# The weights' high and low tiles moved to sixteen places in a 256-byte line

## The chip, the cores and the metric

The kernel runs on one core of one Trainium2 chip. The metric is the device time of one execution in microseconds (us), lower is better. The profile is of one execution, taken by the hardware profiler; the times of the runs were taken without it.

## The reference

The program is a two-layer decoder over 256 tokens of width 2048, in float32: a Mamba-2 layer, a gated MLP with a short causal convolution, a shared key and value projection, an attention layer, and a second gated MLP. Nearly all of the arithmetic is products of the token matrix with weight matrices:

```python
zxbcdt = x @ w_in
...
u = causal_dwconv(x @ w_up, conv_w, conv_b)
gate, val = u[..., :D_FF], u[..., D_FF:]
return (jax.nn.silu(gate) * val) @ w_down
...
kv = h @ w_kv
...
q = (h @ w_q).reshape(Bsz, S, N_HEADS, HEAD_DIM).transpose(2, 0, 1, 3)
```

The inner widths are 10304 for `w_in`, 2 x 5632 for `w_up`, 4096 for `w_kv`, 2048 for the others.

## The kernel before

**High and low parts.** TensorE multiplies in its float32r form, which keeps fewer bits than float32. So every operand is held as two parts, the rounded value (high) and the rest (low), and a product is high x high + low x high + high x low. The activations stand in SBUF as `hT`, `yT`, `gT` or `aT`, 128 partitions with, for each block of 128 rows of the inner dimension, 256 high values (one for each token) and behind them 256 low ones.

**Steps.** The weights come in 880 pieces of 128 x 2 x 512 floats (512 KB, 4096 bytes in a partition), in the order in which they are used. One piece is one step. `load` (L171) issues its DMA into one of four `raw` buffers. `split` (L181) takes one buffer of tag `hi` and one of tag `lo` from the pool `wts`, which has four of each (L95, `LA + 1`), or, for a few steps, free space in `hT` (`spare`). Then ScalarE casts `raw` to the high part (L200) and VectorE subtracts it from `raw` for the low part (L201). `splits` (L204) keeps this up to three steps ahead of the step in work.

**Two kinds of matmul.** A chunk is a block of 512 output columns.

- In mode W, the weights are the stationary operand. `some` (L241) loads 128 x 128 of the high weights and streams high and low activations, 512 columns (L256), or loads 128 x 128 of the low weights and streams the high activations, 256 columns (L259). A piece gives eight of each line, and since every second step turns the order of the two parts round, 16 of one line follow each other; `paired` chunks put two pieces together, and there 32 do.
- In mode X, the activations are the stationary operand and the weights move, 512 columns at a time (256 in the last pieces of a matrix, where `half` is called with `piece`). `half` (L212) issues L222 with the high weights, L223 with the low weights, and L227 with the activations' low part and the high weights.
- One chunk, mode H, has the two parts of 64 columns side by side (`beside`, L262).

Each matmul comes with a weight load of its own: PEld in the profile is the load, PE the matmul.

**What sets the order.** The order of every engine's instructions is written out by hand (`tc.manual_schedule`, L99). The main loop (L1167) walks over the steps, and the dictionaries `pre`, `mid`, `post`, `inner` and `outer` hold the work to be issued around each step; `at(i, f)` puts `f` behind step `i`. Semaphores follow from the tiles that instructions share.

**Addresses.** A tile is a stretch of bytes that is the same in all partitions. The pool `base` lies first: `ident`, `mean`, `cols` (padded to a multiple of 64 floats, `LINE`), `hT`, then the small `mhalf` (8 bytes, for which 32 bytes are set aside), and behind it `tri` and the two buffers of `u`, among others. `wts` follows with four `raw`, four `hi` and four `lo` buffers of 4096 bytes each, then the four `t4k` buffers, then the pool of the stage (`mamba`, `ffn0`, `att`, `ffn1`). The large tiles are multiples of 256 bytes long, so `hT`, `raw`, `hi`, `lo`, `gT`, `yT`, `aT` and `kT` all begin at the same place in a line of 256 bytes, 128 bytes into it; `u` begins 32 bytes further. With the stage `mamba` open, 228,480 bytes of a partition are taken.

**The tile of squares.** In the Mamba stage, for each of eight groups, `x_turn` (L770) writes `xe` (L780), 2048 bytes, which the matmuls of `y_off` (L803) read. Later in the same group, `z_cut` (L829) writes `sq`, 2048 bytes as well, high part by ScalarE (L831) and low part by VectorE (L832), and the matmuls of `z_rms` (L838) read it. The step numbers from the group's start are 13 for `x_turn`, 18 for `y_off`, 22 for `z_cut`, 23 for `z_rms`; the next group starts 16 steps later.

Of the kernel before, what the change touches and what calls it, by code (L numbers as in the profile page):

```python
# [19 lines left out]
F32R = mybir.dt.float32r  # L20
# [4 lines left out]
P = 128  # L25
D = 2048
S = 256
# [12 lines left out]
NC = 512  # L40
# [19 lines left out]
def chunks():  # L60

    z, b, c, dt = 0, 2 * DI, 2 * DI + NG * DS, 2 * DI + 2 * NG * DS

    def some(mode, name, layer, c0, n, nk):
        return [(mode, name, layer, c0 + i * NC, nk, False) for i in range(n)]

    def ffn(layer):
        up = [some(m, "ffn_w_up", layer, c + j * NC, 1, KD)[0] for j in range(DFF // NC)
              for m, c in (("W" if j else "X", 0), ("W", DFF))]
        return up + some("X", "ffn_w_down", layer, 0, 4, KF)  # L70

    out = some("W", "mamba_w_in", 0, b, 2, KD)
    out[0] = out[0][:5] + (True,)
    out += some("H", "mamba_w_in", 0, dt, 1, KD) + some("W", "mamba_w_in", 0, c, 2, KD)
    for g in range(NG):
        out += some("W", "mamba_w_in", 0, DI + g * NC, 1, KD) + some("W", "mamba_w_in", 0, z + g * NC, 1, KD)
    out += some("X", "mamba_w_out", 0, 0, 4, DI // P) + ffn(0)
    out += some("X", "w_kv", None, D, 1, KD) + some("W", "w_kv", None, 0, 4, KD) + some("W", "attn_w_q", 0, 0, 4, KD)
    return out + some("X", "w_kv", None, D + NC, 3, KD) + some("X", "attn_w_o", 0, 0, 4, KD) + ffn(1)
# [12 lines left out]
def yoco_kernel(ctx: ExitStack, tc: tile.TileContext, x, lmg, lmb, lfg, lfb, x_t, columns, w, out):  # L92
    nc = tc.nc
    base = ctx.enter_context(tc.tile_pool(name="base", bufs=1))
    wts = ctx.enter_context(tc.tile_pool(name="wts", bufs=LA + 1))  # L95
# [30 lines left out]
    steps, plan = [], chunks()  # L126
# [44 lines left out]
    def load():  # L171
        i = pos["load"]
        if i >= n_steps:
            return
        pos["load"] += 1
        t = wts.tile([P, 2, NC], F32, tag="raw", name="raw", bufs=RAW)
        for e in (slice(0, 1), slice(1, 2)) if i == 0 else (slice(0, 2),):
            nc.sync.dma_start(t[:, e], w[i][:, e])
        raw_t[i] = t

    def split():  # L181
        i = pos["split"]
        pos["split"] += 1
        t = raw_t.pop(i)
        if i in spare:
            h, l = (bufs["h"][:, k:k + 2].rearrange("p k a t -> p k (a t)") for k in (spare[i], spare[i] + 2))
        else:
            h = wts.tile([P, 2, NC], F32R, tag="hi", name="hi")
            l = wts.tile([P, 2, NC], F32R, tag="lo", name="lo")
        hi_t[i], lo_t[i] = h, l  # L190
        if steps[i][0].mode == "H":
            for a, w in enumerate((h, l)):
                v = t[:, a].rearrange("p (k n) -> p k n", k=8)
                w = w.rearrange("p a (k e n) -> p (a k) e n", e=2, n=NC // 8)
                nc.scalar.copy(w[:, :, 0], v)
                nc.vector.tensor_sub(w[:, :, 1], v, w[:, :, 0].bitcast(F32))
            return load()
        for e in ((0,), (1,)) if i < 2 else ((0, 1),):
            sl = slice(e[0], e[-1] + 1)
            nc.scalar.copy(h[:, sl], t[:, sl])  # L200
            nc.vector.tensor_sub(l[:, sl], t[:, sl], h[:, sl].bitcast(F32))  # L201
        load()

    def splits(i, most=2):  # L204

        for _ in range(1 if steps[i][0] in calm else most):
            j = pos["split"]
            ahead = LA + 1 + sum(i <= k < j for k in spare)
            if j < min(i + ahead, n_steps) and (j in spare or sum(k not in spare for k in hi_t) < LA + 1):
                split()  # L210
# [151 lines left out]
    bufs = {"h": base.tile([P, KD, 2, S], F32R, name="hT")}  # L362
# [179 lines left out]
    def open_pool(name):  # L542
        g = tc.tile_pool(name=name, bufs=1)
        pool[name] = (g, g.__enter__())
        return pool[name][1]
# [26 lines left out]
    calm.append(chB[0])  # L572
    put_x(0)
    split()
    put_x(2)
    split()
    for p in range(2, 8):
        amid(p - 2, put_x, 2 * p)


    mp = open_pool("mamba")
# [123 lines left out]
    G = [dict() for _ in range(NG)]  # L705
# [121 lines left out]
        nc.vector.tensor_add(sz[:, 0], sz[:, 0], sz[:, 1])  # L827

    def z_cut(g):  # L829
        G[g]["sq"] = q = mp.tile([P, 2, S], F32R, tag="sq", name="sq", bufs=1)  # L830
        nc.scalar.copy(q[:, 0], G[g]["sz"][:, 0])  # L831
        nc.vector.tensor_sub(q[:, 1], G[g]["sz"][:, 0], q[:, 0].bitcast(F32))  # L832

# [40 lines left out]
    for g in range(NG):  # L874
# [22 lines left out]
        at(s0 + 20, z_square, g)  # L897
        at(s0 + 21, z_sum, g)
        at(s0 + 22, z_cut, g)
        at(s0 + 23, z_rms, g)  # L900
        at(s0 + 24, z_log, g)
# [217 lines left out]
    for h in range(HEADS):  # L1119
        i, j = divmod(h, 4)  # L1120
# [87 lines left out]
```

## Time and profile before

| | us |
|---|---|
| median of 2 runs | 2539.39 (2539.25 to 2539.53) |
| the profiled execution | 2539.57 |
| its span, first to last instruction | 2537.3 |
| TensorE (PE) busy | 2524.6 |
| weight loads (PEld) busy | 2197.0 |
| VectorE (DVE) busy | 1657.9 |
| ScalarE (ACT) busy | 1365.5 |

The rows that are quoted below come from the following views. The page's first part gives busy time, share of the span and count of each engine; its second part cuts the span in 40 slices of 63.4 us and gives the busy share in tenths. The chain of work that ended last is followed back from the last instruction, each step to what released it. A row of the groups by line reads: line, engine, operation, written tile, read tiles, partitions x elements, count, busy time in us, mean ns of one, then the engine's idle time before it with what ended it. A row of the order of time reads: start in us, time in us from the first start to the last end of so many (x32) merged instructions, engine, line, operation. A matmul's own time overlaps the next one's, so the distance of starts is what counts. A row of one tile's instructions gives duration in ns as min/median/max, then the first and the last start in us. A row of a stretch gives its length, then for PE, PEld, DVE, ACT and POOL the busy us and the count, the granted TensorE clock, the DMA share and GB/s.

### The profile page before, as it was taken

How to read it: one execution, taken by the hardware profiler on the slowest of the kernel's cores; microseconds unless marked ns; L12 is line 12 of the kernel's file. 1: busy time of each engine (PE TensorE's matmuls, PEld its weight loads, DVE VectorE, ACT ScalarE, POOL GpSimd, SP SyncE). 2: the span in 40 equal slices, each digit the busy share in tenths (PEclk: the TensorE clock that was granted, in tenths of full speed). 3: DMA queues.
4: the chain of work that ended last, by engine and by line, in shares of the span. 5: the costliest groups of instructions: out<-in, count | busy, mean ns of one | idle time of the engine just before them, and what ended most of it. 6: DMA issues, size and time to landing. Idle time of an engine off the chain costs nothing.

```text
span 2537.3 us, 36085 instructions
## 1 busy us (share of the span) xinstructions
PE 2524.6 (100%) x13983; PEld 2197.0 (87%) x13983; DVE 1657.9 (65%) x2140; ACT 1365.5 (54%) x1790; POOL 76.6 (3%) x96
## 2 busy tenths in 40 slices
PE   9999999999999999999999999999999999999998
PEld 8888888888888888888888888888888888888887
DVE  7778778755666766666445646645767676765545
ACT  6677787643465555554334445543555555554333
POOL 0000000000200000000000200000200000000001
PEclk9999999999999999999999999999999999999999
DMA  7666665666665555556676655456655555566664
GB/s 253 202 194 199 205 194 186 196 208 223 213 202 189 190 188 189 191 183 200 204 235 203 209 194 168 159 180 227 221 187 193 191 187 190 183 199 200 199 227 163
DMA packets 141739, 502.59 MB, mean 198 GB/s; under 512 B 15856, under 2 KB 16368, under 8 KB 141568
## 3 DMA queue, kind: packets, MB, share of 16 engines
q1 hardware_dynamic: 136448, 482.92, 58.2%
q0 software_dynamic: 4832, 16.85, 2.1%
q8 instruction: 109, 1.79, 0.3%
q14 instruction: 62, 0.51, 0.1%
q10 hardware_dynamic: 288, 0.52, 0.1%
HBM read 491.77 MB, written 8.45 MB: 197 GB/s over the span
## 4 chain that ended last, share of the span: by engine, by line
PE 99%; DMA 0%; DVE 0%; SPq 0%; issue 0%; ACT 0%
PE acc L256 40%; PE acc L259 21%; PE acc L222 11%; PE acc L223 11%; PE acc L227 11%; PE acc L794 1%; PE tp L396 0%; PE tp L227 0%; PE tp L223 0%; PE tp L222 0%; DMA raw<-in_w 0%; PE tp L803 0%; PE acc L777 0%; PE tp L1073 0%; PE tp L1107 0%; PE tp L1099 0%
## 5 line engine op out<-in xcount | busy, mean ns | idle before, releaser
L201 DVE TENSOR_TENSOR lo<-raw,hi 128x1024 fp32r<-128x1024 f32 (+1 forms) x869 | 1059.9, 1225 | 749.6 <-ACT hi L200 616.6
L200 ACT CAST hi<-raw 128x1024 fp32r<-128x1024 f32 (+1 forms) x869 | 908.6, 1048 | 857.8 <-PE acc L227 371.9
L256 PE MATMUL acc<-hT,hi 128*128 128x512 f32 x4480 | 1059.4, 391 | 1.1 <-ACT hi L200 1.1
L256 PEld LDWEIGHTS acc<-hT,hi 128*128 128x128 f32 x4480 | 828.4, 188 | 166.0 <-ACT hi L200 2.0
L259 PEld LDWEIGHTS acc<-hT,lo 128*128 128x128 f32 x4480 | 562.8, 191 | 15.8 <-issue 1.2
L259 PE MATMUL acc<-hT,lo 128*128 128x256 f32 x4480 | 570.6, 283 | 0.0
L223 PE MATMUL acc<-lo,gT 128*128 128x512 f32 (+1 forms) x678 | 254.5, 378 | 0.0
L222 PE MATMUL acc<-hi,gT 128*128 128x512 f32 (+1 forms) x678 | 254.1, 377 | 0.0
L227 PE MATMUL acc<-hi,gT 128*128 128x512 f32 (+1 forms) x678 | 200.7, 377 | 0.0
L222 PEld LDWEIGHTS acc<-hi,gT 128*128 128x128 f32 x678 | 127.6, 188 | 23.2
L223 PEld LDWEIGHTS acc<-lo,gT 128*128 128x128 f32 x678 | 127.6, 188 | 23.1
L227 PEld LDWEIGHTS acc<-hi,gT 128*128 128x128 f32 x678 | 124.8, 188 | 23.8
L223 PE MATMUL acc<-lo,yT 128*128 128x512 f32 (+1 forms) x270 | 98.6, 369 | 0.0
L222 PE MATMUL acc<-hi,yT 128*128 128x512 f32 (+1 forms) x270 | 98.5, 369 | 0.0
L222 PE MATMUL acc<-hi,hT 128*128 128x512 f32 x192 | 78.8, 410 | 0.0
L227 PE MATMUL acc<-hi,yT 128*128 128x512 f32 (+1 forms) x270 | 77.7, 369 | 0.0
L223 PE MATMUL acc<-lo,hT 128*128 128x512 f32 x192 | 75.4, 393 | 0.0
L599 DVE TENSOR_TENSOR u<-u,acc 128x512 f32<-128x512 f32 x108 | 73.4, 681 | 2.3 <-ACT u L598 1.4
L626 DVE SCALAR_TENSOR_TENSOR g<-u,cols,g 128x254 f32<-128x254 f32 (+1 forms) x176 | 73.3, 478 | 0.7 <-ACT g L621 0.7
L626 DVE SCALAR_TENSOR_TENSOR v<-u,cols,v 128x254 f32<-128x254 f32 (+1 forms) x176 | 73.0, 477 | 0.0
L1023 ACT CAST gT<-v 128x512 fp32r<-128x512 f32 x44 | 27.3, 621 | 84.5 <-DVE v L1022 84.5
L458 POOL TENSOR_TENSOR rs<-rs,mhalf 128x1 f32<-128x1 f32 x8 | 7.5, 932 | 2002.2 <-DVE nb L459 2002.2
(223 smaller groups left out, 1911.3 us busy)
## 6 DMA issues: line engine op xcount, KB each, us to landing
raw<-in_w SPq DMA_DIRECT2D x880, 512.0 KB, 3.6
mA<-acum_d POOLq DMA_DIRECT2D x16, 512.0 KB, 6.4
hres<-r POOLq DMA_DIRECT2D x12, 512.0 KB, 6.7
r<-hres SPq DMA_DIRECT2D x12, 512.0 KB, 4.9
eA<-acum_d POOLq DMA_DIRECT2D x16, 128.0 KB, 7.5
r<-in_x SPq DMA_DIRECT2D x4, 512.0 KB, 5.1
gb<-in_ln_mix_g SPq DMA_DIRECT2D x8, 256.0 KB, 4.8
gb<-in_ln_mix_b SPq DMA_DIRECT2D x8, 256.0 KB, 5.0
```

The source lines that it names most:

```text
L200: nc.scalar.copy(h[:, sl], t[:, sl])
L201: nc.vector.tensor_sub(l[:, sl], t[:, sl], h[:, sl].bitcast(F32))
L222: nc.tensor.matmul(a, th, h[:, kk, sl], start=k == 0, stop=False)
L223: nc.tensor.matmul(a, th, l[:, kk, sl], start=False, stop=False)
L227: nc.tensor.matmul(a, ch.x.lo(k)[:, ts], h[:, kk, sl], start=False, stop=k == ch.nk - 1)
L256: nc.tensor.matmul(banks[j], w[:, kk, js], ch.x.both(k), start=begins, stop=ends, skip_group_check=True)
L259: nc.tensor.matmul(banks[j][:, :S], w[:, kk, js], ch.x.hi(k), start=begins, stop=ends, skip_group_check=True)
L458: nc.gpsimd.tensor_tensor(self.rs[:, h, :], self.rs[:, h, :], mhalf[:, 0, :], op=OP.pow)
L599: nc.vector.tensor_add(dst, dst, p[:, :, :S])
L626: nc.vector.scalar_tensor_tensor(d, u[:, i % 2, :S - k], c1(self.at_w, w[n - 1 - k] + self.ia + i), d, op0=OP.mult, op1=OP.add)
L794: nc.tensor.matmul(ps[64 * q:64 * q + 64, c, j * P:(j + 1) * P], G[g]["xdt"][:, c, h * 64:(h + 1) * 64], G[g]["A", c][:, h, :], start=True ...
L1023: nc.scalar.copy(h, v[:, sl])
```

## The change

Every `hi` and `lo` buffer becomes 2 x 512 + 32 floats long, 4224 bytes in place of 4096. The tile that is used in it begins `at` floats in, where `at` is 0, 4, 8 ... 28 and goes on by 4 floats (16 bytes) every second step. Since 4224 is 16 lines of 256 bytes and a half, neighbouring buffers are also half a line apart, so that with both, sixteen steps in a row stand at sixteen places of a line, all of them multiples of 16 bytes. The high and the low part of a step are at the same place. The chunk of mode H uses `at` 0, and the steps in `spare` are not touched. Then `sq` no longer has a buffer of its own and takes the tag of `xe`, whose single buffer the two now share; this gives back 2048 bytes in a partition, where the eight longer buffers take 1024. All tiles behind `wts` lie 1024 bytes further, at the same place in a line as before. The order of the instructions on every engine and the semaphores that they wait for are the same in both kernels.

```diff
@@ -185,8 +185,10 @@
         if i in spare:
             h, l = (bufs["h"][:, k:k + 2].rearrange("p k a t -> p k (a t)") for k in (spare[i], spare[i] + 2))
         else:
-            h = wts.tile([P, 2, NC], F32R, tag="hi", name="hi")
-            l = wts.tile([P, 2, NC], F32R, tag="lo", name="lo")
+
+            at = 4 * (i // 2 % 8) if steps[i][0].mode != "H" else 0
+            h, l = (wts.tile([P, 2 * NC + 32], F32R, tag=n, name=n)[:, at:at + 2 * NC].rearrange("p (a n) -> p a n", a=2)
+                    for n in ("hi", "lo"))
         hi_t[i], lo_t[i] = h, l
         if steps[i][0].mode == "H":
             for a, w in enumerate((h, l)):
@@ -827,7 +829,7 @@
         nc.vector.tensor_add(sz[:, 0], sz[:, 0], sz[:, 1])
 
     def z_cut(g):
-        G[g]["sq"] = q = mp.tile([P, 2, S], F32R, tag="sq", name="sq", bufs=1)
+        G[g]["sq"] = q = mp.tile([P, 2, S], F32R, tag="xe", name="sq", bufs=1)
         nc.scalar.copy(q[:, 0], G[g]["sz"][:, 0])
         nc.vector.tensor_sub(q[:, 1], G[g]["sz"][:, 0], q[:, 0].bitcast(F32))
```

## The prediction

> **What bounds the kernel now.** I read the page's busy shares first, then the chain of work that ended last, then the order of time on TensorE in one stretch of each of the two kinds of matmul.
>
> ```profile
> PE 2524.6 (100%) x13983; PEld 2197.0 (87%) x13983; DVE 1657.9 (65%) x2140; ACT 1365.5 (54%) x1790; POOL 76.6 (3%) x96
> ...
> DVE  7778778755666766666445646645767676765545
> ...
> PEclk9999999999999999999999999999999999999999
> ...
> PE 99%; DMA 0%; DVE 0%; SPq 0%; issue 0%; ACT 0%
> PE acc L256 40%; PE acc L259 21%; PE acc L222 11%; PE acc L223 11%; PE acc L227 11%; PE acc L794 1%; PE tp L396 0%; PE tp L227 0%; PE tp L223 0%; PE tp L222 0%; DMA raw<-in_w 0%; PE tp L803 0%; PE acc L777 0%; PE tp L1073 0%; PE tp L1107 0%; PE tp L1099 0%
> ```
>
> The reader is to see that 99% of the chain is TensorE, that its clock is granted in full, and that five lines hold 94%: L256 and L259, where the weights are the stationary operand, and L222, L223 and L227, where they are the moving one. A busy TensorE need not be at its peak, so the next question is what sets the distance from one matmul to the next. First a stretch of the first kind, then one of the second:
>
> ```profile
> 2000.48 4.00 PE L259 MATMUL acc<-hT,lo 128*128 128x256 f32 x32
> 2004.31 7.44 PE L256 MATMUL acc<-hT,hi 128*128 128x512 f32 x32
> 2011.59 4.00 PE L259 MATMUL acc<-hT,lo 128*128 128x256 f32 x32
> 2015.42 0.86 PE L256 MATMUL acc<-hT,hi 128*128 128x512 f32 x3
> ```
>
> ```profile
> 1206.36 0.61 PE L227 MATMUL acc<-hi,gT 128*128 128x512 f32 x2
> ...
> 1207.72 0.39 PE L227 MATMUL acc<-hi,gT 128*128 128x512 f32 x1
> ```
>
> 32 low-part matmuls of 256 columns take 2004.31 - 2000.48 = 3.83 us, 119.7 ns each, and again 3.83 us from 2011.59. Of the second kind, six of 512 columns take 1207.72 - 1206.36 = 1.36 us, 226.7 ns each. So 256 more columns cost 107.0 ns, 0.418 ns a column, and what is left over is 119.7 - 107.0 = **12.7 ns for each matmul, whatever its width**. The high-part run of 32 takes 2011.59 - 2004.31 = 7.28 us, 227.5 ns each, nearly the same. The four buffers of the weights take turns through these runs, so nothing above the place in a line shows in the distance.
>
> **What the change does, part by part.** Order, waits, sizes, shapes and DMAs of every instruction stay as they were; only addresses move. Each high and low tile becomes 1056 floats long, 4224 bytes = 16 lines of 256 + 128 bytes, so neighbouring buffers stand half a line apart, and the data begins another 16 x (step // 2 mod 8) bytes in. That gives sixteen places, all multiples of 16 bytes, where before all tiles began at one. These groups count what is touched:
>
> ```profile
> L201 DVE TENSOR_TENSOR lo<-raw,hi 128x1024 fp32r<-128x1024 f32 (+1 forms) x869 | 1059.9, 1225 | 749.6 <-ACT hi L200 616.6
> L200 ACT CAST hi<-raw 128x1024 fp32r<-128x1024 f32 (+1 forms) x869 | 908.6, 1048 | 857.8 <-PE acc L227 371.9
> L256 PEld LDWEIGHTS acc<-hT,hi 128*128 128x128 f32 x4480 | 828.4, 188 | 166.0 <-ACT hi L200 2.0
> L259 PEld LDWEIGHTS acc<-hT,lo 128*128 128x128 f32 x4480 | 562.8, 191 | 15.8 <-issue 1.2
> L222 PE MATMUL acc<-hi,gT 128*128 128x512 f32 (+1 forms) x678 | 254.1, 377 | 0.0
> L222 PE MATMUL acc<-hi,yT 128*128 128x512 f32 (+1 forms) x270 | 98.5, 369 | 0.0
> L222 PE MATMUL acc<-hi,hT 128*128 128x512 f32 x192 | 78.8, 410 | 0.0
> L222 PE MATMUL acc<-hi,aT 128*128 128x512 f32 (+1 forms) x126 | 46.9, 376 | 0.0
> L222 PE MATMUL tp<-hi,gT 128*128 128x256 f32 x72 | 18.7, 282 | 0.0
> ```
>
> *Weight loads of L256 and L259*: 2 x 4480 = 8960 reads of 512 bytes. *Moving reads of L222, L223 and L227*: 678 + 270 + 192 + 126 + 72 = 1338 on each line, 4014 reads of 1 or 2 KB. Together 12,974 of the 13,983 matmuls read something moved. No row of before has a TensorE read at another place, so the cost has to be bounded. Below nothing: a gain can at most take the 12.7 ns that isn't columns. Above: a read that begins inside some unit of the memory touches one unit more. Places are multiples of 16 bytes, so a unit of 16 costs nothing, and with a unit of 64 bytes, 12 of 16 places pay. For a moving read that is 16 columns, 16 x 0.418 = 6.7 ns. For a weight load it is one unit in eight of a stream that repeats every 119.7 ns, at most 15.0 ns, and only where the load has no slack: a load begins with each matmul, and in L256's runs it has 227.5 - 119.7 = 107.8 ns to spare, so only L259's 4480 can show it. I take **0** for both, because the rows nearest in kind, the two engines that do work at several places, show none:
>
> ```profile
> L599 DVE TENSOR_TENSOR u<-u,acc 128x512 f32<-128x512 f32 x108 | 73.4, 681 | 2.3 <-ACT u L598 1.4
> L401 DVE TENSOR_TENSOR hT<-tp,hT 128x512 fp32r<-128x512 f32 x24 | 16.3, 680 | 1.7 <-ACT hT L400 1.7
> L626 DVE SCALAR_TENSOR_TENSOR g<-u,cols,g 128x255 f32<-128x255 f32 x88 | 38.6, 479 | 0.7 <-ACT g L621 0.7
> L626 DVE SCALAR_TENSOR_TENSOR g<-u,cols,g 128x254 f32<-128x254 f32 x88 | 38.3, 477 | 0.0
> L598 ACT COPY u<-acc 128x512 f32<-128x512 f32 x108 | 62.0, 575 | 0.0
> L598 ACT COPY kT<-acc 128x512 f32<-128x512 f32 x8 | 4.6, 575 | 0.0
> ```
>
> Tile u is allocated behind the 8-byte mhalf and so begins 32 bytes off the places of hT, kT and the weights; yet an operation into u takes 681 ns against 680 into hT, and ScalarE's copy 575 ns into either. L626 writes one or two floats off any line, and 255 and 254 elements take 479 and 477 ns.
>
> [...]
>
> *The 869 casts and subtractions.* By the rows above, 0. The cover, should they stretch: in the densest stretch,
>
> ```profile
> 317.00:381.00 64.00, 64.00 (x405) 56.97 (x404) 51.16 (x74) 52.33 (x85) 3.03 (x4) 1.00 0.60 194
> ```
>
> VectorE is busy 51.16 of 64 us and ScalarE 52.33 of 64, beside a full TensorE; the weights are cut up to three steps ahead.
>
> *The squares' tile in xe's buffer.* Its user of before and its next user:
>
> ```profile
> L803 PE MATMUL tp<-bc,xe x8: 272/275/275, 304.0 to 304.8; 128*128 128x128 f32 x8
> L780 DVE TENSOR_TENSOR xe<-xdt,aux x2: 677/678/680, 294.5 to 343.8; 128x512 f32<-128x512 f32 x2
> ```
>
> ```profile
> L838 PE MATMUL tp<-sq,mean x2: 278/280/283, 320.9 to 321.0; 128*128 128x256 f32 x2
> L831 ACT CAST sq<-sz x1: 407/407/407, 317.6 to 317.6; 128x256 fp32r<-128x256 f32 x1
> ```
>
> The last matmul that reads xe starts at 304.8 and the squares are written at 317.6, 12.5 us after its end; the squares are last read at 321.0 and xe is written anew at 343.8. Both gaps are hidden by order alone; without that order the cost would be a ScalarE wait of under a step. Cost 0.
>
> **The sum.** 0 + 0 + 0 against the profiled execution's 2539.57 us (span 2537.3), which stands 0.2 us above the median of the runs, 2539.39. I forecast 2539.4 us.
>
> **The rivals.**
>
> *A, slower: an off-line read costs TensorE a unit more.* With a unit of 64 bytes: 4480 x 12/16 x 15.0 ns = 50.4 us for L259's loads, 4014 x 12/16 x 6.7 ns = 20.2 us for the moving reads, 70.6 us, 2610 us in all; loads alone 2590, moving reads alone 2560. For it: the loads of L259 come every 119.7 ns and last 191 ns where those of L256 last 188, so they are the nearer to being a limit. Against it: the 12.7 ns are the same there as with 512 columns, where a load has 107 ns to spare, so the load doesn't bind today. It passes 2% (50.8 us) from 50.8 / 12,974 = 3.9 ns a matmul.
>
> [...]
>
> *B, faster: the 12.7 ns are two reads meeting at the same place.* Now the stationary and the moving operand both begin at one place in a line. If that made the fixed part, fifteen of sixteen steps would shed it: 12,974 x 15/16 x 12.7 ns = 154 us, 2385 us. Against it: meeting reads would meet again at every line, so the loss should grow with the columns, and it is the same 12.7 ns with both widths. It also passes 2% from 3.9 ns a matmul.
>
> [...]
>
> *C, slower: casts and subtractions stretch until VectorE is the limit.* In 317 to 381 us VectorE has 12.8 us left; L201's share of VectorE over all is 1059.9 / 1657.9 = 64%, so about 33 of the 51 us, and it decides from about 12.8 / 33 = 39% more per operation. At double the time the eight slices that the page shows at 7 or 8 tenths ahead of the first 5 (8 x 63.4 = 507 us) would lose (33 - 12.8) / 64 of themselves, 160 us: 2700 us. Against it: 681 and 680 ns above.
>
> *D, the change does not do what it says*, because the allocator packs or pads otherwise: it would read the same 2539.4 us and is no case of its own; the time can't tell it from the forecast.
>
> **How the numbers follow.** Forecast (nothing moves, 2534 to 2545) 0.72; A 0.14, of which 0.06 past 2%; B 0.09, of which 0.05 past 2%; C 0.05, of which 0.04 past 2%. So faster by over 2% 0.05, slower 0.06 + 0.04 = 0.10, within 2% 0.85, and 2% is about what a measurement of this kernel is read by. The range runs from 2520, an eighth of B's gain (1.6 ns a matmul), to 2590, where A has the loads alone; it leaves out the large ends of A, B and C, 0.15.
>
> **What would show it.** Right: the 32 matmuls of L259 still take 3.83 us, six of L227, L222 and L223 1.36 us, L200 and L201 1048 and 1225 ns. A is shown by L259's runs, longer for twelve places of sixteen and not for the other four, with L256's unchanged; B by runs shorter at all but one place; C by L201's mean above 1700 ns and TensorE idle time released by L201. What would make the prediction wrong is a TensorE that minds places which ScalarE and VectorE don't, for no row of before has tried it.

## The result and the profile after

The changed kernel takes 2565.59 us (2565.57 to 2565.61, 2 runs) against 2539.39 us: 26.2 us more, a ratio of 1.0102 with a 95% interval of 1.0086 to 1.0119. That is slower by 1%, within 2%, and inside the range on record, but not by the mechanism that the forecast rests on: the forecast was that nothing moves. The profiled execution took 2565.61 us, its span 2563.3.

The page of the changed kernel, where lines behind the edit stand two further than before (L256 is now L258, L259 is L261, L222, L223 and L227 are L224, L225 and L229, L200 and L201 are L202 and L203):

```profile
PE 2550.4 (99%) x13983; PEld 2189.8 (85%) x13983; DVE 1658.4 (65%) x2140; ACT 1363.4 (53%) x1790; POOL 76.4 (3%) x96
...
PE 99%; DMA 0%; DVE 0%; SPq 0%; issue 0%; ACT 0%
...
L203 DVE TENSOR_TENSOR lo<-raw,hi 128x1024 fp32r<-128x1024 f32 (+1 forms) x869 | 1060.2, 1225 | 772.2 <-ACT hi L202 635.6
L202 ACT CAST hi<-raw 128x1024 fp32r<-128x1024 f32 (+1 forms) x869 | 906.0, 1045 | 885.2 <-PE acc L229 380.4
L258 PE MATMUL acc<-hT,hi 128*128 128x512 f32 x4480 | 1077.4, 395 | 1.5 <-ACT hi L202 1.5
L258 PEld LDWEIGHTS acc<-hT,hi 128*128 128x128 f32 x4480 | 827.8, 188 | 182.5 <-ACT hi L202 2.3
L261 PEld LDWEIGHTS acc<-hT,lo 128*128 128x128 f32 x4480 | 556.7, 188 | 17.4 <-issue 1.2
L261 PE MATMUL acc<-hT,lo 128*128 128x256 f32 x4480 | 564.5, 281 | 0.0
```

The two matmul rows of the kernel before, for comparison:

```profile
L256 PE MATMUL acc<-hT,hi 128*128 128x512 f32 x4480 | 1059.4, 391 | 1.1 <-ACT hi L200 1.1
L259 PE MATMUL acc<-hT,lo 128*128 128x256 f32 x4480 | 570.6, 283 | 0.0
```

TensorE is still 99% of the chain, and its busy time has grown by 2550.4 - 2524.6 = 25.8 us, nearly all of the change. ScalarE and VectorE take what they took, 1045 ns (1048 before) and 1225 ns an operation. The matmuls with the high parts in mode W have grown by 18.0 us and those with the low parts have **shrunk** by 6.1 us; the remaining 14 us are mode X, whose distances from start to start sum up to 884.9 us before and 899.1 us after. No weight load lasts longer: L261's even went from 191 to 188 ns.

The order of time on TensorE in the same two stretches as before, mode W and mode X:

```profile
2001.23 7.59 PE L258 MATMUL acc<-hT,hi 128*128 128x512 f32 x32
2008.66 3.95 PE L261 MATMUL acc<-hT,lo 128*128 128x256 f32 x32
2012.44 7.60 PE L258 MATMUL acc<-hT,hi 128*128 128x512 f32 x32
```

```profile
1204.23 0.62 PE L229 MATMUL acc<-hi,gT 128*128 128x512 f32 x2
...
1205.62 0.62 PE L229 MATMUL acc<-hi,gT 128*128 128x512 f32 x2
```

32 high-part matmuls take 2008.66 - 2001.23 = 7.43 us, 232.2 ns each in place of 227.5; 32 low-part ones 3.78 us, 118.1 in place of 119.7; six of mode X 1.39 us, 231.7 in place of 226.7. The engines wait for nothing new; the 512-column matmuls simply start some 5 ns later behind the one before, and the 256-column ones 1.6 ns sooner.

### The profile page after: what moved, and what is told of

Read it like the earlier page. It is cut to its first block, busy times and chain, and to the rows that moved or that the text cites. A ratio compares the mean times of both kernels' runs of the same rounds, so it can differ in the third digit from the quotient of the medians.

```text
span 2563.3 us, 36085 instructions
## 1 busy us (share of the span) xinstructions
PE 2550.4 (99%) x13983; PEld 2189.8 (85%) x13983; DVE 1658.4 (65%) x2140; ACT 1363.4 (53%) x1790; POOL 76.4 (3%) x96
## 4 chain that ended last, share of the span: by engine, by line
PE 99%; DMA 0%; DVE 0%; SPq 0%; issue 0%; ACT 0%
PE acc L258 41%; PE acc L261 21%; PE acc L224 11%; PE acc L225 11%; PE acc L229 11%; PE acc L796 1%; PE tp L398 0%; PE tp L225 0%; PE tp L229 0%; PE tp L224 0%; PE tp L805 0%; PE acc L779 0%; PE tp L1075 0%; PE tp L1109 0%; DMA raw<-in_w 0%; PE tp L1101 0%
## 5 line engine op out<-in xcount | busy, mean ns | idle before, releaser
L203 DVE TENSOR_TENSOR lo<-raw,hi 128x1024 fp32r<-128x1024 f32 (+1 forms) x869 | 1060.2, 1225 | 772.2 <-ACT hi L202 635.6
L202 ACT CAST hi<-raw 128x1024 fp32r<-128x1024 f32 (+1 forms) x869 | 906.0, 1045 | 885.2 <-PE acc L229 380.4
L258 PE MATMUL acc<-hT,hi 128*128 128x512 f32 x4480 | 1077.4, 395 | 1.5 <-ACT hi L202 1.5
L258 PEld LDWEIGHTS acc<-hT,hi 128*128 128x128 f32 x4480 | 827.8, 188 | 182.5 <-ACT hi L202 2.3
L261 PEld LDWEIGHTS acc<-hT,lo 128*128 128x128 f32 x4480 | 556.7, 188 | 17.4 <-issue 1.2
L261 PE MATMUL acc<-hT,lo 128*128 128x256 f32 x4480 | 564.5, 281 | 0.0
L225 PE MATMUL acc<-lo,gT 128*128 128x512 f32 (+1 forms) x678 | 257.0, 382 | 0.0
L224 PE MATMUL acc<-hi,gT 128*128 128x512 f32 (+1 forms) x678 | 256.9, 381 | 0.0
L229 PE MATMUL acc<-hi,gT 128*128 128x512 f32 (+1 forms) x678 | 203.4, 381 | 0.0
L224 PEld LDWEIGHTS acc<-hi,gT 128*128 128x128 f32 x678 | 127.5, 188 | 26.0
L225 PEld LDWEIGHTS acc<-lo,gT 128*128 128x128 f32 x678 | 127.4, 188 | 26.0
L229 PEld LDWEIGHTS acc<-hi,gT 128*128 128x128 f32 x678 | 124.7, 188 | 26.5
L224 PE MATMUL acc<-hi,yT 128*128 128x512 f32 (+1 forms) x270 | 99.5, 373 | 0.0
L225 PE MATMUL acc<-lo,yT 128*128 128x512 f32 (+1 forms) x270 | 99.3, 372 | 0.0
L224 PE MATMUL acc<-hi,hT 128*128 128x512 f32 x192 | 79.2, 413 | 0.0
L229 PE MATMUL acc<-hi,yT 128*128 128x512 f32 (+1 forms) x270 | 78.6, 372 | 0.0
L225 PE MATMUL acc<-lo,hT 128*128 128x512 f32 x192 | 76.1, 396 | 0.0
```

The source lines that it names most:

```text
L224: nc.tensor.matmul(a, th, h[:, kk, sl], start=k == 0, stop=False)
L225: nc.tensor.matmul(a, th, l[:, kk, sl], start=False, stop=False)
L229: nc.tensor.matmul(a, ch.x.lo(k)[:, ts], h[:, kk, sl], start=False, stop=k == ch.nk - 1)
L258: nc.tensor.matmul(banks[j], w[:, kk, js], ch.x.both(k), start=begins, stop=ends, skip_group_check=True)
L261: nc.tensor.matmul(banks[j][:, :S], w[:, kk, js], ch.x.hi(k), start=begins, stop=ends, skip_group_check=True)
```

## The experiments

Two theories at the start. **P**: the place of TensorE's weights against its activations sets the distance of its matmuls, whatever the other steps do. **C**: the distance suffers because the place changes from step to step. "Place" means bytes, within a line of 256, by which the weights begin further than the activations; "distance" is the time from the start of one matmul to the start of the next. `at` counts floats of 4 bytes, so `at` 8 is place 32. The diffs show only the lines that set the places. In all kernels below, unless said otherwise, the buffers are `2 * NC + 64` floats (17 lines of 256 bytes), so that all four begin at one place, the squares share xe's buffer as in the change, and `tri` is taken from the pool `mp` for room. Each is compared with the kernel before on the same chip; that ran at 2538.79 to 2539.09 us (medians of its groups of runs).

**The same place, only size and buffers changed.**

```diff
-            at = 4 * (i // 2 % 8) if steps[i][0].mode != "H" else 0
+            at = 0
```

> The buffers are 17 lines of 256 bytes long (4352 bytes), all weights begin at the old place (place 0: the place at which the activations begin), the squares share xe's buffer, and the triangle's tile lies in the stage's pool. Theory P (the place of TensorE's weight operand against its activation operand sets the distance of matmuls): nothing but size has moved, 2539.4 us within 1. Theory C (what costs is that the place changes from step to step): the same. A third view, that the longer buffers or the shared buffer cost the 26 us: about 2565 us.

Measured: 2539.15 us, ratio 1.000 (0.9991 to 1.0009). The longer buffers and the shared buffer of the squares cost nothing; the addresses are left.

**All weights 32 bytes further, for good.**

```diff
+            at = 8 if steps[i][0].mode != "H" else 0
```

> As the one before, but the weights of all steps begin 32 bytes further (place 32), activations as ever: the place differs from that of the activations and never changes. Theory P, from the place-32 steps of the changed kernel (L256's matmuls 233 ns apart in place of 228, L259's 118.2 in place of 119.9, the 512-column ones of the other kind 233 in place of 227): 4480 x 5 - 4480 x 1.7 + about 3400 x 5.8 = 34 us more, 2573 us. Theory C: no change of place, 2539.4 us within 2.

Measured: 2574.96 us, ratio 1.0142 (1.0127 to 1.0157). Its order of time:

```profile
2004.23 3.95 PE L261 MATMUL acc<-hT,lo 128*128 128x256 f32 x32
2008.03 7.62 PE L258 MATMUL acc<-hT,hi 128*128 128x512 f32 x32
2015.49 3.95 PE L261 MATMUL acc<-hT,lo 128*128 128x256 f32 x32
```

7.46 us for 32 high parts is 233.1 ns each, 3.80 us for 32 low parts 118.8 ns. The place never changes here, and the loss is larger than the change's own. Theory C falls.

**Everything 32 bytes further**, with `at` 0 in all steps.

```diff
+    base.tile([P, 8], F32, name="shift")
     ident = base.tile([P, P], F32, name="ident")
```

> A 32-byte tile ahead of everything else shifts activations, weights and raw pieces alike by 32 bytes, so that nothing moves against anything. If it is the place of weights against activations that counts: 2539.4 us within 1. If it is a place in the line as such (32 bytes off where all stood): as with the weights alone at place 32, about 2573 us.

Measured: 2538.78 us, ratio 1.000 (0.999 to 1.0009). So the old place in the line, as such, does not matter for this shift: what counts is where something stands *against* something else.

**Each of the sixteen places kept for eight steps.**

```diff
+            at = 4 * (i // 8 % 16) if steps[i][0].mode != "H" else 0
```

> All sixteen places again, but each is kept for eight steps (64 matmuls of each part in mode W) before the next. Theory P: the mean over the places is what it was, 2565 us within 5, and each place shows a distance of its own that lasts. Theory C: an eighth of the changes of place, 2539.4 + 26 / 8 = 2543 us, and within eight steps the distance returns to 226.7 and 119.9 ns.

Measured: 2565.69 us, ratio 1.0105 (1.009 to 1.012), the change's time to 0.1 us, with an eighth of the changes of place. Theory C falls here too. In this run a place shows a distance of its own that lasts as long as the place does. Mean distances in ns at eight of the sixteen places, without the first eight matmuls of each run of one line (in mode X, of each stay at a place); they are good to some tenths of a ns:

| place | high, 512 columns | low, 256 columns | mode X, 512 columns |
|---|---|---|---|
| 0 | 226.7 | 120.0 | (227.4) |
| 16 | 233.4 | 118.2 | |
| 32 | 233.4 | 118.4 | 233.3 |
| 64 | 233.2 | 113.7 | 230.5 |
| 96 | 234.3 | 118.0 | 233.4 |
| 128 | 233.2 | 118.5 | 232.4 |
| 192 | 230.3 | 117.0 | 232.9 |
| 240 | 228.0 | 119.3 | |

No step of mode X has place 0, 16 or 240 in this run; the 227.4 ns are those of the kernel before. Place 0, where the kernel before stands, is the best of those shown for 512 columns (226.7 ns) and the worst of them for 256 (120.0 ns). That is the whole of the result: two kinds lose, the third gains.

**Raw pieces and weights both 32 bytes further.** Buffers of 4096 bytes; 32 bytes are set aside ahead of the first raw buffer and 224 behind the last low one, so that everything behind stays at its place.

```diff
+        if i == 0:
+            wts.tile([P, 8], F32, tag="shift", name="shift", bufs=1)
         t = wts.tile([P, 2, NC], F32, tag="raw", name="raw", bufs=RAW)
...
+            if i == 0:
+                wts.tile([P, 56], F32, tag="rest", name="rest", bufs=1)
```

> Raw pieces and weights both begin 32 bytes further, so that ScalarE and VectorE read and write at one place as before, and only TensorE's two operands stand 32 bytes apart. Theory P, TensorE's own two reads: as with the weights alone at place 32, 2575 us within 3. If it is the cast and the subtraction that collide with TensorE when they read at one place and write at another: 2539 us.

Measured: 2574.89 us, ratio 1.0143 (1.0126 to 1.016), as with the weights alone (2574.96 us). ScalarE and VectorE now read and write at one place, and it changes nothing. With the run that moved everything, this leaves TensorE's own two operands, the stationary and the moving one, as the pair that matters. The traces agree that no other engine is needed for it. Take the mode X matmuls of 512 columns during which, and for 0.2 us ahead of which, ScalarE, VectorE and GpSimd do nothing: their mean distance is 226.7 ns in the kernel before (34 of them) and 232.8 ns with all weights at place 32 (28 of them). For the high parts of mode W it is 226.9 ns (56) against 235.0 ns (55).

**Steps of 4 bytes**, to see whether the distance goes by the exact place (one execution, with its profile). Mode W alone:

```diff
+                    for n, at in (("hi", i // 8 % 16 if steps[i][0].mode == "W" else 0), ("lo", 8 + i // 8 % 16 if steps[i][0].mode == "W" else 0)))
```

> Mode W only: the high parts at places 0, 4, 8 ... 60 bytes and the low parts at 32, 36 ... 92 bytes, each kept for eight steps; mode X at place 0. [...] If it goes by the exact place: sixteen different distances. [...]

Measured: 2550.16 us. High parts at 0, 4, 8 and 12 bytes: 226.8, 232.3, 230.7 and 232.2 ns. Low parts at 48, 52, 56 and 60: 117.9, 113.4, 117.8 and 119.4. Neighbours within 16 bytes differ by up to 6 ns, nearly as much as any two places of the table, and two places off a multiple of 16 (52 and 76) are the fastest for the low parts. So a beginning off a multiple of 16 bytes costs nothing of its own: 113.4 ns at 52 against 117.9 at 48. In this run both parts move together, so what one place does alone is left to the runs below.

**Low parts at place 64, the best in the table (113.7 ns).**

```diff
+                    for n, at in (("hi", 0), ("lo", 16 if steps[i][0].mode == "W" else 0)))
```

> Buffers of 17 lines, all at the place of the activations but the low parts of mode W, which begin 64 bytes further. Theory P, from the run that kept each place for eight steps (L259's matmuls 113.65 ns apart at place 64 against 119.96 at place 0): 4480 x 6.3 = 28 us less, 2511 us, faster than before. If instead every place but 0 costs, or if a second place beside the first undoes the gain: 2539 us or more.

Measured: 2529.75 us, ratio 0.9964 (0.9951 to 0.9977). Faster than both kernels, but by 9 us, not 28 (L257 and L260 are here what L256 and L259 are in the kernel before):

```profile
2003.87 3.93 PE L260 MATMUL acc<-hT,lo 128*128 128x256 f32 x32
2007.64 7.44 PE L257 MATMUL acc<-hT,hi 128*128 128x512 f32 x32
2014.91 3.93 PE L260 MATMUL acc<-hT,lo 128*128 128x256 f32 x32
```

3.77 us for 32 is 117.8 ns, where the run by eight steps had shown 113.7 at this place. Theory P as stated, one distance for one place, falls with this. In that run the high parts had stood at 64 too. So:

**Both parts of mode W at place 64** (one execution, with its profile).

```diff
+                    for n, at in (("hi", 16 if steps[i][0].mode == "W" else 0), ("lo", 16 if steps[i][0].mode == "W" else 0)))
```

> Both parts of mode W at place 64, mode X at place 0. If the distance follows what stood before as well as the place: L259's matmuls 113.65 ns apart, as where both stood at 64 for eight steps, L256's 233.2; 4480 x 5.2 - 4480 x 6 = 4 us less than 2539, 2535 us. If the place alone sets it and 113.65 was an accident of the short stay: L259's at 117.6 and 2539 + 4480 x (5.2 - 2.2) = 2552 us.

Measured: 2537.14 us.

```profile
2002.31 7.62 PE L257 MATMUL acc<-hT,hi 128*128 128x512 f32 x32
2009.78 3.79 PE L260 MATMUL acc<-hT,lo 128*128 128x256 f32 x32
2013.41 7.62 PE L257 MATMUL acc<-hT,hi 128*128 128x512 f32 x32
```

The low parts now take 2013.41 - 2009.78 = 3.63 us for 32, 113.4 ns, at the same place where they took 117.8, and only the place of the high parts, which run ahead of them, differs. So a place has more than one lasting distance. The run through all places, below, shows both in one trace: in step 640, eight low parts at place 64 that follow directly on low parts at place 60 take 0.91 us, 113 to 115 ns each, and those of the next step at place 64, behind high parts at place 0, 118 ns each.

**Low parts at all 64 places, and then high parts** (one execution each, with its profile; the first line below is the edit of the one, the other two that of the other).

```diff
+                    for n, at in (("hi", 0), ("lo", i // 8 % 64 if steps[i][0].mode == "W" else 0)))
...
+            m, n = steps[i][0].mode, i // 4 % 64
+            ats = (i // 8 % 64, 19) if m == "W" else (n, n) if m == "X" else (0, 0)
```

> High parts at place 0, low parts of mode W at all 64 places that are multiples of 4 bytes, each kept for eight steps; mode X at place 0. If the distance follows the place alone: the values of the earlier runs, 113.4 to 120 ns for L259, place 64 at 113.65 ns. If it also follows what stood before (with the low parts alone at place 64, L259's matmuls were 117.6 ns apart in place of 113.65): place 64 at 117.6, and other places that do reach 113.4 from high parts at place 0, or none. Total: 4480 x about 2 ns less than 2539, some 2530 us.

Measured: 2533.00 us, where about 2530 was expected. Behind high parts at place 0, the low parts stay at 117.7 ns at place 64, but come down to 113.4 at 76, 88 and 180 after two to four matmuls; the other places reached give 115.7 to about 121. Place 52, 113.4 ns in the run by steps of 4 bytes, gives 120 here. And with the high parts fixed, places 72 and 76, which lie within the same 16 bytes, still differ: 118.3 and 113.4 ns.

> Mode W: low parts at place 76, high parts at all 64 places of 4 bytes, each kept for eight steps; mode X: both parts at all 64 places, each kept for four steps. The low parts' best distance is 113.4 ns, 6.6 ns under the 120.0 of place 0. If 512-column matmuls have such places too, some high places show about 226.7 - 6.6 = 220 ns; if 226.7 is their best, none is under it. Total, since most places known for the high parts cost 5 ns and those of mode X 5 ns: 2565 us, within 10.

Measured: 2553.06 us, a little under the expected 2555 to 2575. At the places that mode W reached (none from 200 to 244), 512 columns never have a mean under 226.7 ns; 0, 120 and 252 reach it, and so does 132 after its first eight matmuls; most stand at 230 to 234, the worst, 164, at about 237. Mode X also has its best near 227 ns and reaches about 240 at 68 and 196.

**Low parts at place 76.**

```diff
+                    for n, at in (("hi", 0), ("lo", 19 if steps[i][0].mode == "W" else 0)))
```

> High parts at place 0, low parts of mode W at place 76 throughout. From the run over all places: 114.3 ns a matmul of L259 with the transitions, against 119.9: 4480 x 5.6 = 25 us less, 2514 us, faster than before and than the low parts at place 64 (2529.75). If long stays lose the short distance again: 2530 us.

Measured: 2513.73 us, ratio 0.990 (0.9884 to 0.9917), 25 us under the kernel before and 52 under the change.

```profile
2001.85 3.80 PE L260 MATMUL acc<-hT,lo 128*128 128x256 f32 x32
2005.49 7.44 PE L257 MATMUL acc<-hT,hi 128*128 128x512 f32 x32
2012.77 3.80 PE L260 MATMUL acc<-hT,lo 128*128 128x256 f32 x32
```

3.64 us for 32 low parts, 113.8 ns with the first few; 7.28 us for the high ones, as before. The matmuls and their order are those of the kernel before; 4480 operands begin 76 bytes further.

## Why the prediction was right or wrong

*The bound* was read rightly: TensorE's distance from start to start set the time before and after, and all of the 26 us lies there.

*"I take 0 for both, because the rows nearest in kind, the two engines that do work at several places, show none"* is the step that failed. The rows were right about their own engines: L203 and L202 stayed at 1225 and 1045 ns, and moving the raw pieces along changed nothing. But they say nothing about TensorE, where the place of one operand against the other changed the distance. The term taken as 0 measured 26.0 us of span, on average 26.0 / 12,974 = 2.0 ns for each of the matmuls that the prediction counts as moved: 18.0 us in L258, 14 us in mode X, less 6.1 us in L261. The text had named this as what would make it wrong, since no row of before had tried it; so the price was unknown, and 0 was a choice that no row of TensorE supported. That the time still fell inside the range is luck: the upper part of the range was there for rival A, and what happened is not rival A.

*Rival A* had the sign and a fitting size, but not the mechanism. It asked for L259's runs longer, L256's unchanged and four places in sixteen free. L259's got shorter, L256's longer, and places 64, 128 and 192 cost the 512 columns 233.2, 233.2 and 230.3 ns. No unit of 64 bytes whose border is crossed explains that, and places 4 bytes apart, inside one such unit, differ as well.

*Rival B* named the right pair, TensorE's two operands, and had the wrong sign for most of it: off place 0 it had every moved matmul gain, and only the 256-column ones did. The argument against it, and against A, that both widths show the same 12.7 ns, was empty: the 12.7 ns come from a line laid through just these two widths, so both had to show them. The runs decide: at place 64 the 512-column matmuls of mode W lose 6.5 ns and the 256-column ones gain 2 to 7. The fixed 12.7 ns that it hoped to shed are not the same thing in both: the 256-column ones shed up to 6.6 ns (120.0 to 113.4), the 512-column ones nothing at any place tried. Whether the two reads collide in the memory, or the one is timed by the other inside TensorE, no row here shows, and why a stream keeps one of two distances stays open as well.

In the time of this kernel the two operands are not independent: with the weights alone 32 bytes further, the matmuls of 512 columns stood 233.1 ns apart in mode W in place of 227.5, and 1.40 us for six, 233.3 ns, in mode X in place of 226.7; with both operands 32 bytes further the time was 2538.78 us against 2538.90.

The units of 16 and 64 bytes with which the prediction bounds the cost, and rival A's 50.4 and 20.2 us with them, are the author's assumption. No run shows such a unit: at 48, 52, 56 and 60 bytes the low parts take 117.9, 113.4, 117.8 and 119.4 ns.

*The squares in xe's buffer and the longer buffers*: 0, as forecast, by the run with all at the same place (2539.15 against 2538.90 us). *Rival C* did not occur: L203's mean stayed at 1225 ns. *Rival D* is excluded by the addresses' effect itself.

## What to carry to other kernels

Where TensorE is the bound and every matmul loads new weights, read the distance from start to start for each width in the order of time; the place of the stationary operand against the moving one is a free parameter in it, worth +1.4% to -1.0% here. Spreading over sixteen places only averaged good and bad ones (2565.59 us, where one place for all gave 2539.15 or 2574.96); try single places for each kind of matmul, in the real sequence, since a place that is best in one order of work is not in another: low parts at 64 took 113.4 ns behind high parts at 64, but 117.8 behind high parts at 0, where 76 took 113.8. A row of one engine that is insensitive to something is no price for another engine.

## What the runs showed of the hardware that was not expected

The distance of matmuls in this kernel depends on the relative place of the two operands, down to steps of 4 bytes: between 113.4 and about 121 ns for 256 columns and between 226.7 and about 237 ns for 512 in mode W, with the granted clock at 0.998 to 0.999 throughout. It has a memory: at place 64 the same 32 matmuls take 3.77 or 3.63 us, by what ran ahead of them. The means often hide a short pattern that repeats: low parts at place 52 behind high parts at 0 start 120, 118, 122, 120, 118, 122 ns apart and so on, and high parts at place 164 go 256, 237, 230, 229, 234 ns and begin again. And shifting both operands alike by 32 bytes leaves the time where it was to about 0.1 us (2538.78 against 2538.90).
